# First products of a decoder trunk: modulation and weight parts spread over the engines in another way, and a planner with other costs

## The chip, the cores and the metric

The kernel runs on 1 core of one Trainium2 chip. A time is the device time of one execution in microseconds (us). The median of three runs before the change is 1367.15 us. The engines are PE (matrix products), DVE and POOL (elementwise vector work), ACT (activation functions, also copies with scale and bias) and SP, which issues the transfers (DMA).

## The reference

Two layers of a decoder over x (512 tokens by 1024 features, float32), then a last norm:

```python
mod = (c @ w_ada + b_ada)[:, None, :]
sh_m, sc_m, g_m, sh_f, sc_f, g_f = jnp.split(mod, 6, axis=-1)
h = rms_norm(x) * (1 + sc_m) + sh_m
proj = h @ w_in
x_lru, q_down, kv_down, k_rope, gate_a, gate_b = jnp.split(proj, IN_SPLIT_POINTS, axis=-1)
y_a = rg_lru(causal_depthwise_conv(x_lru, conv_w, conv_b), positions, ...)
y_b = mla(q_down, kv_down, k_rope, cos, sin, q_norm_g, kv_norm_g, w_uq, w_ukv)
y = jax.nn.sigmoid(gate_a) * y_a + jax.nn.sigmoid(gate_b) * y_b
x = x + g_m * (y @ w_out)
h = rms_norm(x) * (1 + sc_f) + sh_f
gate, up = jnp.split(h @ w_ffn_in, 2, axis=-1)
x = x + g_f * ((jax.nn.silu(gate) * up) @ w_ffn_out)
```

`rg_lru` is a gated recurrence over the tokens, `mla` a causal attention with 8 heads whose queries and keys come from narrow projections (`q_down` 256 columns, `kv_down` 128, `k_rope` 64). c is one vector of 1024, so `mod` is one vector of 6144 per layer: scale, shift and gate for both halves of a layer.

## The kernel before, in words

All activations lie feature-major: tile j holds 128 features by 512 tokens. Every product is done with operands split in two: a value is hi + lo, both in the engine's fast 32-bit type (`fp32r`), and `mm3` (line 567) issues three products of 128x512 per 128 rows of weights: hi by hi, hi by lo, lo by hi. `split` (line 558) makes the parts: ACT copies to hi, and a subtraction on DVE gives lo.

**Who sets the order.** The program doesn't issue its engine calls at once. A `Recorder` notes them, `order()` (line 302) plays them through on a model of the engines and lists for each engine, among the calls that are ready and have buffers, the one with the longest remaining path, and `issue()` issues them in that order (so every instruction carries line 503 before and 513 after). `cost()` (line 267) holds the durations of the model: a product of 512 columns, an elementwise step by its width, a transfer, an ACT table load. While the model's PE is idle before the first products are through, `fill()` puts in a product on zeros of 128x256 in bf16, the `fill` rows, whose results nobody reads. In the issued order each engine takes its instructions strictly in turn.

**The first products** (`first_products`, line 990). For the first layer the eight feature tiles of x are taken in order. Tile j needs `xn` (x times `rst`, the reciprocal root mean square of each token), its scale and shift, and the rows of `w_in` for x_lru tiles 0 and 1 and all narrow projections (704 columns). These are 17 products per tile into six accumulators, which stay open over all eight tiles. The scale and shift are made just before, for one or two tiles at a time, from the columns of `w_ada` that the tiles take (`first_mods`, line 948; 32 transfers of 256 KB into `wa`). The table `FIRST` has one entry per step: first tile, number of tiles, and two letters for scale and shift. Letter P: PE multiplies eight blocks of 128x128 of `wa` with c (`pt<-cols1,wa`, 128x64, in float32; each appears as two records). Letter V: DVE adds up the rows weighted by c (`wacc`: one `tensor_scalar` and seven `scalar_tensor_tensor` of 128x128 for one tile, 128x256 for two), and PE only sums over the partitions with one product per tile (`pt<-ones,wacc`). A small DVE step then adds the bias (`mod0_1` is the scale, `mod0_0` the shift).

`full_h` (line 998) turns `xn` into h: ACT writes the scaled and shifted tile once rounded (`hh`) and once in full (`xn`), and DVE subtracts (`hl`). `w_first` (line 618) loads and splits the weights: ACT writes `whi`, and the two subtractions (128x640 into `wlo`, 128x64 into a side column of `whi`) run on DVE for tile 0 and on POOL for tiles 1 to 7 (`WLO_G`). There are three raw weight buffers and three pairs of hi and lo.

**Beside and behind them.** `tables` (line 1058), placed after the third step, loads small parameters, makes the rotary tables (three steps of 128x512 on POOL) and `scol`, a chain of 22 steps of 128x16 on POOL with a reciprocal and one `scalar_tensor_tensor` (`w16_0`, in the trace `w`) on DVE. Then follow the statistics of the narrow projections (`sacc`, `rs2`), more columns of `w_in`, the convolution `xc`, the recurrence's gates and scans (`ri`), and the attention, interleaved by a script of steps (`SCRIPT`, line 75). In the background DVE adds up further modulation columns (`macc`, from `graw` transfers).

Of the kernel before, what the change touches and what calls it, by code (L numbers as in the profile page):

```python
# [78 lines left out]
FIRST = ((0, 1, "PP"), (1, 1, "VP"), (2, 2, "PV"), (4, 2, "VV"), (6, 2, "VV"))  # L79
A2_G = True  # L80
HI_G = ()
WLO_G = (1, 2, 3, 4, 5, 6, 7)
# [10 lines left out]

# [1 line left out]
# The body below records its engine calls in program order. order() then lists them by a  # L95
# simulated greedy schedule: each engine takes, of the calls whose operands are ready and whose
# tiles have a free buffer, the one with the longest remaining path. The calls are issued in
# that order, and Tile puts in the waits that the data needs.
# [17 lines left out]
class Op:  # L116
    __slots__ = ("eng", "call", "a", "k", "dur", "preds", "succs", "allocs", "tiles", "tail", "table", "idx",
                 "npred", "ready", "bytes", "live")


class Ref:
    """A view of a tile that is made when the first call on it is issued."""

    def __init__(self, root, steps, dtype, part, free, off):
        self.root, self.steps, self.dtype = root, steps, dtype
        self.part, self.free, self.off = part, free, off  # (start, count), [(stride, count)], column
# [67 lines left out]
class Recorder:  # L194
# [25 lines left out]
    def add(self, eng, real, method, a, k):  # L220
# [43 lines left out]
        op.dur = self.cost(op, eng, method, a, k, outs, ins)  # L264
        self.ops.append(op)

    def cost(self, op, eng, method, a, k, outs, ins):
# [8 lines left out]
        if eng == "PE":  # L276
            if method == "transpose":
                return 107.0
            lhs, rhs = a[1], a[2]
            n = free(rhs)  # L280
            op.live = n > 32
            return max(207.0, n * 1.667) if lhs.dtype == F32 else max(53.0, n * 0.417)
# [19 lines left out]
    def order(self):  # L302
# [8 lines left out]
        # longest remaining path, with the products chained in program order  # L311
# [14 lines left out]
        # users of each tile  # L326
# [12 lines left out]
        def fits(o):  # L339
            """a free buffer for each new tile, and one more for each tile that the program makes before it"""  # L340
# [17 lines left out]
        # the clock of the tensor engine: full speed after a window full of work, half after an idle one  # L358
# [21 lines left out]
        dma_free = 0.0  # L380
        res = []
# [8 lines left out]
        def fill():  # L390
            """keeps the clock of the idle tensor engine up until the first products are through"""
# [8 lines left out]
        while count < n:  # L400
            for e in ENGINES:
# [49 lines left out]
                if e == "PE":  # L451
                    d = clock(now, d, o.live)
                if e == "ACT" and o.table and table not in o.table:
                    d += TABLE_LOAD
                    table = o.table[0]
# [62 lines left out]
def trunk(  # L518
# [36 lines left out]
    def f(ap):  # L555
        return ap.bitcast(F32)
# [5 lines left out]
    def mm2(ps, wboth, xh, xl, start, stop):  # L562
        """high and low parts of 64 columns at once: their products lie in the two halves of the partitions"""
# [26 lines left out]
    def w_cols(src, nk=KD, on_g=False, raws=None):  # L590
        """src: rows (k p), 128 columns; gives [(hi, lo)] over k, and adds the blocks as loaded to raws"""
# [12 lines left out]
    def w_krope(l):  # L604
        """rotary key columns: high and low parts side by side"""
# [12 lines left out]
    def w_first(l, j, keep):  # L618
        """rows of feature tile j: columns of x_lru tiles 0 and 1 and of all the down projections; gives the
        five (hi, lo), the rotary key columns' high and low parts side by side, and the columns as loaded"""  # L620
# [23 lines left out]
    def w_lru(l, n0):  # L644
        """input and recurrence gate weights of blocks n0..n0+3"""
# [8 lines left out]
    def w_rope(l, g):  # L654
        """rotary query weights of heads 4g..4g+3, as [k][half][head, 32]"""
# [16 lines left out]
    def w_pair(l, p2):  # L672
        """query (no rotary) and key/value weights of heads 2*p2, 2*p2+1"""
# [49 lines left out]
    mods = {}  # L723

    def mod_steps(l, s):
        """generator: one segment (1024 columns) of c @ w_ada[l] + b_ada[l], as columns [128, 8]"""
# [25 lines left out]
    def mod_products(l, s):  # L752
        """the same segment on the tensor engine: w_ada stationary, c moving"""
# [21 lines left out]
    # ---- work for the tensor engine while it waits at the start, so that its clock stays up  # L775
# [32 lines left out]
    def rsqrt(r, ssum, n, w, eps):  # L808
        """r = (ssum / n + EPS) ** -0.5: the reciprocal of what the Sqrt table gives, and one Newton step"""
# [11 lines left out]
    def sqrt_eps():  # L821
        """EPS as a column by the Sqrt table, not before the last call so far: the table is there
        when the statistics are"""
# [6 lines left out]
    class Stat:  # L830
# [13 lines left out]
        def finish(self, cs, n, sbuf=False):  # L844
            """rstd broadcast over partitions, in columns cs of PSUM or of a tile in SBUF"""
# [26 lines left out]
    # Across a norm the products go on before its statistics are there: the first units take x times  # L872
    # the scale, and their results are multiplied by rstd and get the shift's share as a column.
    class Ahead:
# [12 lines left out]
        def units(self, srcs):  # L887
            """products with the column blocks srcs: PSUM tiles, and the shift's columns"""
# [21 lines left out]
    def gemm_units(units, xh, xl, get_w, done):  # L910
        """units: (m, column slice); weights of m by get_w(m): list over k of (hi, lo) APs"""
# [637 lines left out]
```

## Time and profile before

| | |
|---|---|
| runs | 1367.56, 1367.15, 1366.49 us; median 1367.15 us |
| profiled execution, span from first to last instruction | 1361.9 us |
| its own device time | not given beside the span; the median of the runs lies 5.25 us above it |
| mean granted PE clock | 0.995 of full speed |
| busy: PE, DVE, ACT, POOL | 98%, 64%, 46%, 16% of the span |
| instructions | 17108 |
| PE filler products | 57 |

PE is busy nearly all the time, so its rows show the run of the program from start to end: transposes of x to 16 us, the first products to 67 us, the first layer to about 680 us, the second to the end. A busy PE isn't at its peak everywhere: products overlap, and the distance from one start to the next says more than the duration of one. Idle time on another engine matters only where PE waits for what that engine makes. In timelines a row stands for one instruction or several of a kind in a row (x2, x3); the square brackets give the idle time just before it and what ended it.

### The profile page before, as it was taken

What the parts mean: (1) busy time and instruction counts of PE and PEld (TensorE: products, weight loads), DVE (VectorE), ACT (ScalarE), POOL (GpSimd) and SP (SyncE); (2) the same over time, 40 slices, a digit from 0 to 9 for tenths busy, and PEclk for the clock granted to TensorE, in tenths of its full rate; (3) what the DMA queues carried; (4) which work ended last, traced back from release to release, by engine and by line L of the source; (5) the groups of instructions that cost most, each with busy time, mean ns of one, the idle gap of its engine ahead of it and who ended that gap; (6) DMA issues with size and microseconds to landing.
All of it is one profiled execution on the core that took longest, in us unless ns stands there. A gap on an engine that the chain in (4) does not pass through costs nothing.

```text
span 1361.9 us, 17108 instructions
## 1 busy us (share of the span) xinstructions
PE 1339.6 (98%) x6330; PEld 1117.8 (82%) x6330; DVE 872.4 (64%) x1478; ACT 623.5 (46%) x963; POOL 213.2 (16%) x238
## 2 busy tenths in 40 slices
PE   8999989999999999999999999999999999999997
PEld 7788878887888888888888888888888888888887
DVE  5898799788856455556869887667673333333344
ACT  5585856644432222322356767855452322232223
POOL 1613334413000000000040243413400000000000
PEclk9999989999999999999999999999999999999999
DMA  9636344334655556555635333311433323433232
GB/s 300 200 96 168 103 124 140 124 117 137 194 182 164 163 159 206 178 170 184 203 86 141 92 86 100 94 47 47 124 89 98 89 75 104 120 93 95 77 88 81
DMA packets 251297, 174.92 MB, mean 128 GB/s; under 512 B 12767, under 2 KB 235341, under 8 KB 251213
## 3 DMA queue, kind: packets, MB, share of 16 engines
q1 hardware_dynamic: 251212, 173.82, 42.3%
q8 instruction: 50, 0.82, 0.2%
q14 instruction: 35, 0.28, 0.1%
HBM read 167.50 MB, written 2.10 MB: 125 GB/s over the span
## 4 chain that ended last, share of the span: by engine, by line
PE 84%; DVE 6%; DMA 5%; issue 2%; POOL 1%; ACT 1%; SPq 1%; ACTq 0%; DVEq 0%; POOLq 0%
PE mm L503 75%; PE s L503 4%; PE o L503 3%; DMA graw<-in_w_ada_dram 2%; PE pt L503 2%; DMA wa<-in_w_ada_dram 2%; DMA raw<-in_w_in_dram 1%; DVE macc L503 1%; DVE ri L503 1%; DVE wlo L503 1%; DVE xc L503 1%; POOL w L503 1%; DVE wacc L503 1%; SPq L503 1%; DVE sc L503 0%
## 5 line engine op out<-in xcount | busy, mean ns | idle before, releaser
L503 ACT ACTIVATE whi<-raw 128x1024 fp32r<-128x1024 f32 (+2 forms) x226 | 219.7, 973 | 581.3 <-PE mm L503 371.1
L503 DVE TENSOR_TENSOR wlo<-raw,whi 128x1024 fp32r<-128x1024 f32 (+2 forms) x218 | 249.3, 1145 | 205.5 <-ACT whi L503 201.2
L503 PE MATMUL mm<-fh,wlo 128*128 128x512 f32 x672 | 261.9, 390 | 0.0
L503 PE MATMUL mm<-fh,whi 128*128 128x512 f32 x672 | 261.7, 389 | 0.0
L503 PE MATMUL mm<-fl,whi 128*128 128x512 f32 x672 | 261.6, 389 | 0.0
L503 PE MATMUL mm<-hh,whi 128*128 128x512 f32 x408 | 161.3, 396 | 0.0
L503 PE MATMUL mm<-hl,whi 128*128 128x512 f32 x408 | 160.2, 393 | 0.0
L503 PE MATMUL mm<-hh,wlo 128*128 128x512 f32 x400 | 156.3, 391 | 0.0
L503 PEld LDWEIGHTS mm<-fl,whi 128*128 128x128 f32 x672 | 126.1, 188 | 26.4 <-DVE fl L503 0.2
L503 PEld LDWEIGHTS mm<-fh,wlo 128*128 128x128 f32 x672 | 126.1, 188 | 26.4 <-DVE wlo L503 0.3
L503 PEld LDWEIGHTS mm<-fh,whi 128*128 128x128 f32 x672 | 126.2, 188 | 26.0
L503 PE MATMUL mm<-ah,whi 128*128 128x512 f32 (+1 forms) x363 | 139.7, 385 | 0.0
L503 PE MATMUL mm<-ah,wlo 128*128 128x512 f32 (+1 forms) x363 | 139.3, 384 | 0.0
L503 PE MATMUL mm<-al,whi 128*128 128x512 f32 (+1 forms) x363 | 139.0, 383 | 0.0
L503 DVE SCALAR_TENSOR_TENSOR macc<-graw,cols,macc 128x512 f32<-128x512 f32 x140 | 103.8, 777 | 24.1 <-DMA graw<-in_w_ada_dram 23.7
L503 DVE TENSOR_TENSOR sg<-sg,mm 128x512 f32<-128x512 f32 x42 | 28.9, 688 | 111.1 <-PE mm L503 111.1
L503 PEld LDWEIGHTS mm<-hl,whi 128*128 128x128 f32 x408 | 77.0, 189 | 15.5 <-DVE hl L503 0.5
L503 PEld LDWEIGHTS mm<-hh,whi 128*128 128x128 f32 x408 | 77.0, 189 | 15.1 <-DVE whi L503 0.2
L503 PEld LDWEIGHTS mm<-hh,wlo 128*128 128x128 f32 x400 | 75.4, 189 | 15.8 <-POOL wlo L503 0.3
L503 PEld LDWEIGHTS mm<-ah,wlo 128*128 128x128 f32 x363 | 68.2, 188 | 13.3
L503 PEld LDWEIGHTS mm<-al,whi 128*128 128x128 f32 x363 | 68.2, 188 | 13.1
L503 PEld LDWEIGHTS mm<-ah,whi 128*128 128x128 f32 x363 | 68.2, 188 | 13.1
(266 smaller groups left out, 2173.9 us busy)
## 6 DMA issues: line engine op xcount, KB each, us to landing
raw<-in_w_ffn_in_dram SPq DMA_DIRECT2D x88, 512.0 KB, 3.9
graw<-in_w_ada_dram SPq DMA_DIRECT2D x80, 512.0 KB, 4.8
raw<-in_w_in_dram SPq DMA_DIRECT2D x49, 512.0 KB, 4.0
raw<-in_w_ffn_out_dram SPq DMA_DIRECT2D x32, 384.0 KB, 3.5
raw<-in_w_ffn_out_dram SPq DMA_DIRECT2D x32, 320.0 KB, 3.2
wa<-in_w_ada_dram SPq DMA_DIRECT2D x32, 256.0 KB, 5.6
raw<-in_w_out_dram SPq DMA_DIRECT2D x16, 512.0 KB, 3.9
raw<-in_w_uq_dram SPq DMA_DIRECT2D x24, 128.0 KB, 3.5
```

Of the source, the lines that this page charges most:

```text
L503: o.call(*(real(v) for v in o.a), **{k: real(v) for k, v in o.k.items()})
```

## The change

In `FIRST` the scale of step (1,1) and the shift of step (4,2) go from V to P, and in step (2,2) the two letters change places. `WLO_G` is empty, so all lo parts of the first weights are made on DVE. `full_h` makes the modulated tile in one DVE step with two column operands, then splits it as weights are split. The planner's costs of products are others, and a DVE or POOL step with two tensor inputs from SBUF now waits, in the model, for such a step on the other of the two. Comments and docstrings go, which moves line numbers only.

```diff
-FIRST = ((0, 1, "PP"), (1, 1, "VP"), (2, 2, "PV"), (4, 2, "VV"), (6, 2, "VV"))
+FIRST = ((0, 1, 'PP'), (1, 1, 'PP'), (2, 2, 'VP'), (4, 2, 'VP'), (6, 2, 'VV'))
...
-WLO_G = (1, 2, 3, 4, 5, 6, 7)
+WLO_G = ()
...
+        op.shared = eng in ("DVE", "POOL") and method in ("tensor_tensor", "scalar_tensor_tensor") and 2 == sum(
+            isinstance(x, Ref) and x.root.tag not in BANKS and x.shape[-1] > 1 for x in ins
+        )
...
-            return max(207.0, n * 1.667) if lhs.dtype == F32 else max(53.0, n * 0.417)
+            if lhs.dtype == F32:
+                return max(107.0, n * 1.667)
+            return n * 0.417 if lhs.dtype == BF16 else max(106.0, n * 0.417 + 10.3)
...
+        shared = {"DVE": 0.0, "POOL": 0.0}
...
+                if o.shared:
+                    other = "POOL" if e == "DVE" else "DVE"
+                    d += max(0.0, shared[other] - now)
+                    shared[e] = now + d
...
-            A.activation(hh[j], xn[j], AF.Identity, bias=sh, scale=sc)
-            A.activation(xn[j], xn[j], AF.Identity, bias=sh, scale=sc)
-            V.tensor_tensor(hl[j], xn[j], f(hh[j]), ALU.subtract)
+            V.tensor_scalar(xn[j], xn[j], sc, sh, ALU.mult, ALU.add)
+            split(hh[j], hl[j], xn[j])
```

By the tables PE has 64 modulation products of 128x64 instead of 40 and 8 of `ones` with `wacc` instead of 11; DVE has 32 `wacc` steps, all of 128x256, instead of 8 of 128x128 and 40 of 128x256. The planner makes the whole order anew. The filler products become 84 instead of 57, and ACT's table loads 56 instead of 51. Three places show what moves.

PE at the start of tile 1 (tile names: `hh_38`, `hl_46` are the parts of h, `mm_53` to `s_56` accumulators, `pt` the modulation's). Before:

```order
L503 MATMUL pt_81_371<-cols1_150,wa_85_265 128x64 x2
L503 MATMUL pt_81_371<-cols1_150,wa_82_234 128x64 x2
L503 MATMUL pt_81_371<-cols1_150,wa_83_240 128x64 x2
L503 MATMUL pt_81_371<-cols1_150,wa_84_252 128x64 x2
L503 MATMUL pt_81_371<-cols1_150,wa_85_265 128x64 x2
L503 MATMUL mm_53_345<-hh_38_363,whi_92_412 128x512
L503 MATMUL mm_53_345<-hl_46_390,whi_92_412 128x512
L503 MATMUL mm_53_345<-hh_38_363,wlo_93_425 128x512
L503 MATMUL mm_54_350<-hh_38_363,whi_92_412 128x512
L503 MATMUL mm_54_350<-hl_46_390,whi_92_412 128x512
L503 MATMUL pt_81_371<-ones_83,wacc_90_352 128x64 x2
L503 MATMUL mm_54_350<-hh_38_363,wlo_93_425 128x512
```

Now, where the first row shown is the last of 21 fillers that stand between the last products of tile 0 and tile 1:

```order
L513 MATMUL fill_4_87<-fill_x_75,fill_w_77 128x256
L513 MATMUL pt_80_458<-ones_83,wacc_85_360 128x64 x2
L513 MATMUL mm_53_365<-hh_38_400,whi_91_440 128x512
L513 MATMUL mm_53_365<-hl_46_418,whi_91_440 128x512
L513 MATMUL mm_54_369<-hh_38_400,whi_91_440 128x512
L513 MATMUL mm_54_369<-hl_46_418,whi_91_440 128x512
L513 MATMUL s_55_373<-hh_38_400,whi_91_440 128x512
L513 MATMUL mm_53_365<-hh_38_400,wlo_92_466 128x512
L513 MATMUL pt_80_458<-cols1_150,wa_86_257 128x64 x2
L513 MATMUL pt_80_458<-cols1_150,wa_87_267 128x64 x2
L513 MATMUL pt_80_458<-cols1_150,wa_88_283 128x64 x2
L513 MATMUL pt_80_458<-cols1_150,wa_89_302 128x64 x2
```

Before, 14 modulation products stood together ahead of the tile (seven rows of two, the last five are shown). Now fillers stand there, the two `ones` products (one row) have moved ahead of the tile, and 16 modulation products for the shift of tiles 2 and 3 (eight rows, four of them shown) come after its sixth product. The lo parts that POOL's queue held before stand on DVE among its `wacc` steps, and POOL's queue begins with the rotary tables.

DVE behind the first products, before (`w16_0` is the step that needs the chain on POOL, `sacc` the statistics that PE waits for next):

```order
L503 SCALAR_TENSOR_TENSOR xc_172_784<-xl_171_769,cols2_638,xc_172_784 128x510
L503 SCALAR_TENSOR_TENSOR w16_0_643<-w16_4_71,w16_0_643 128x16
L503 SCALAR_TENSOR_TENSOR xc_172_784<-xl_171_769,cols2_638,xc_172_784 128x509
L503 TENSOR_TENSOR sacc_148_810<-sacc_148_810,sq_149_815 128x512
L503 TENSOR_TENSOR xcl_174_836<-xc_172_784,xch_173_829 128x512
L503 TENSOR_TENSOR wlo_204_851<-raw_202_747,whi_203_840 128x1024
```

Now:

```order
L513 SCALAR_TENSOR_TENSOR xc_170_801<-xl_169_786,cols2_685,xc_170_801 128x509
L513 TENSOR_TENSOR sacc_146_825<-sacc_146_825,sq_147_831 128x512
L513 TENSOR_TENSOR wlo_202_855<-raw_200_767,whi_201_844 128x1024
L513 TENSOR_TENSOR xcl_172_875<-xc_170_801,xch_171_862 128x512
L513 RECIPROCAL rs2_149_897<-hs_150_870 128x4
L513 TENSOR_SCALAR ms_151_902<-o_148_859 128x4
L513 RECIPROCAL rs2_160_904<-hs_161_894 128x4
L513 SCALAR_TENSOR_TENSOR nt_152_907<-rs2_149_897 128x4
L513 TENSOR_SCALAR ms_162_909<-o_159_867 128x4
L513 SCALAR_TENSOR_TENSOR nt_163_911<-rs2_160_904 128x4
L513 TENSOR_TENSOR nt_152_907<-nt_152_907,ms_151_902 128x4
L513 SCALAR_TENSOR_TENSOR w16_0_692<-w16_4_71,w16_0_692 128x16
```

The step on `w16_0` stands no longer ahead of `sacc`, but ten rows behind it, among the statistics `rs2`.

DVE around 175 us of the trace before (`ri<-a2` are elementwise steps of the recurrence, `ri<-a` with `a` the scans, `xc<-mm` the convolution, which frees an accumulator of PE, `macc` the background modulation). Before:

```order
L503 SCALAR_TENSOR_TENSOR macc_169_1270<-graw_388_1825,cols1_150,macc_169_1270 128x512 x2
L503 SCALAR_TENSOR_TENSOR ri_258_1235<-a2_390_1850,ri_258_1235 128x512
L503 TENSOR_TENSOR xcl_382_1886<-xc_380_1828,xch_381_1878 128x512
L503 TENSOR_SCALAR sg_354_1847<-sg_354_1847 128x512
L503 SCALAR_TENSOR_TENSOR ri_212_1082<-a_383_1806,ri_212_1082 128x512
L503 SCALAR_TENSOR_TENSOR xc_395_1889<-mm_394_1823,cols2_638,xc_395_1889 128x511
L503 SCALAR_TENSOR_TENSOR ri_255_1228<-a_364_1656,ri_255_1228 128x512
L503 SCALAR_TENSOR_TENSOR xc_395_1889<-mm_394_1823,cols2_638,xc_395_1889 128x510
L503 TENSOR_TENSOR wlo_476_1917<-raw_474_1864,whi_475_1901 128x1024
L503 SCALAR_TENSOR_TENSOR xc_395_1889<-mm_394_1823,cols2_638,xc_395_1889 128x509
```

Now:

```order
L513 SCALAR_TENSOR_TENSOR xc_378_1868<-mm_377_1790,cols2_685,xc_378_1868 128x510
L513 SCALAR_TENSOR_TENSOR ri_256_1267<-a2_388_1873,ri_256_1267 128x512
L513 SCALAR_TENSOR_TENSOR xc_378_1868<-mm_377_1790,cols2_685,xc_378_1868 128x509
L513 SCALAR_TENSOR_TENSOR macc_167_1374<-graw_386_1862,cols1_150,macc_167_1374 128x512 x2
L513 TENSOR_TENSOR xcl_380_1934<-xc_378_1868,xch_379_1917 128x512
L513 SCALAR_TENSOR_TENSOR xc_393_1910<-mm_392_1860,cols2_685,xc_393_1910 128x511
L513 TENSOR_TENSOR wlo_474_1955<-raw_472_1883,whi_473_1922 128x1024
L513 SCALAR_TENSOR_TENSOR xc_393_1910<-mm_392_1860,cols2_685,xc_393_1910 128x510
L513 SCALAR_TENSOR_TENSOR ri_210_1110<-a_381_1803,ri_210_1110 128x512
L513 SCALAR_TENSOR_TENSOR xc_393_1910<-mm_392_1860,cols2_685,xc_393_1910 128x509
```

The two scans ahead of the last `xc` of tile `xc_395` have become one, of another tile, between its last two parts; the other has gone further back.

## Rows read from the trace of the kernel before

**Rows 1.** The page, part 1: busy time, share of the span, instructions of each engine.
```profile
PE 1339.6 (98%) x6330; PEld 1117.8 (82%) x6330; DVE 872.4 (64%) x1478; ACT 623.5 (46%) x963; POOL 213.2 (16%) x238
```

**Rows 2.** Three windows: busy us and instructions by engine, PE's granted clock, DMA share and rate.
```profile
core 0: us, PE busy (x) PEld busy (x) DVE busy (x) ACT busy (x) POOL busy (x), PEclk, DMA share, GB/s
28.50:46.50 18.00, 15.80 (x82) 11.85 (x81) 18.00 (x40) 8.42 (x13) 6.20 (x7) 1.00 0.92 287
184.00:191.00 7.00, 6.47 (x16) 4.34 (x15) 7.00 (x13) 5.21 (x7) 2.71 (x2) 0.52 0.86 284
1100.00:1150.00 50.00, 50.00 (x222) 41.39 (x221) 15.95 (x21) 10.64 (x14) 0.00 (x0) 1.00 0.31 89
```

**Rows 3.** PE's waits, 0 to 350 us: waited for, us in total, times, longest.
```profile
PE mm L503 <- DVE xc L503: 3.0, 1, 3.0
PE pt L503 <- DVE cols L503: 2.1, 1, 2.1
PE pt L503 <- DVE mod L503: 2.1, 2, 1.8
...
PE o L503 <- DVE sacc L503: 1.0, 1, 1.0
```

**Rows 4.** Groups on DVE, then POOL, 20 to 76 us: busy us, mean ns, idle before.
```profile
L503 DVE SCALAR_TENSOR_TENSOR wacc<-wa,cols,wacc 128x256 f32<-128x256 f32 x35 | 22.9, 700 | 0.1
...
L503 DVE TENSOR_TENSOR wlo<-raw,whi 128x640 fp32r<-128x640 f32 x1 | 0.8, 818 | 0.0
...
L503 DVE TENSOR_SCALAR ang<-ang 128x512 f32<-128x512 f32 x1 | 0.4, 446 | 0.0
...
L503 POOL TENSOR_SCALAR kk<-kk 128x512 f32<-128x512 f32 x1 | 0.9, 941 | 0.1
```

**Rows 5.** Timeline of DVE, then POOL, around 27 us: start, duration.
```profile
26.55 0.48 DVE L503 SCALAR_TENSOR_TENSOR wacc<-wa,cols,wacc 128x256 f32<-128x256 f32 x1
...
27.54 1.77 DVE L503 SCALAR_TENSOR_TENSOR wacc<-wa,cols,wacc 128x256 f32<-128x256 f32 x1
...
27.34 1.70 POOL L503 TENSOR_TENSOR wlo<-raw,whi 128x640 fp32r<-128x640 f32 x1 [26.51 <-ACT whi L503]
```

**Rows 6.** PE's timeline at places in the first products and behind them.
```profile
20.98 0.71 PE L503 MATMUL mm<-hh,whi 128*128 128x512 f32 x2
...
25.43 3.23 PE L503 MATMUL pt<-cols,wa 128*128 128x64 f32 x28
28.47 0.48 PE L503 MATMUL mm<-hh,whi 128*128 128x512 f32 x1
...
45.01 1.70 PE L503 MATMUL fill<-fill_x,fill_w 128*128 128x256 bf16 x14
...
52.88 0.66 PE L503 MATMUL pt<-ones,wacc 128*128 128x64 f32 x4 [2.15 <-DVE cols L503]
...
67.15 0.48 PE L503 MATMUL mm<-hh,whi 128*128 128x512 f32 x1
...
75.99 1.03 PE L503 MATMUL s<-ident,rs 128*128 128x128 f32 x8
```

**Rows 7.** Timeline of POOL, then DVE: scol's chain and the step that waits for it.
```profile
58.00 0.54 POOL L503 TENSOR_TENSOR w<-w,w 128x16 f32<-128x16 f32 x1
...
69.63 0.18 DVE L503 SCALAR_TENSOR_TENSOR w<-w,w 128x16 f32<-128x16 f32 x1 [1.41 <-POOL w L503]
```

**Rows 8.** DVE's timeline, 163 to 184 us.
```profile
164.69 1.75 DVE L503 SCALAR_TENSOR_TENSOR macc<-graw,cols,macc 128x512 f32<-128x512 f32 x2 [2.03 <-DMA graw<-in_w_ada_dram]
...
175.61 2.30 DVE L503 TENSOR_TENSOR_SCAN ri<-a,ri 128x512 f32<-128x512 f32 x1
...
182.16 0.73 DVE L503 SCALAR_TENSOR_TENSOR xc<-mm,cols,xc 128x509 f32<-128x509 f32 x1
```

**Rows 9.** ACT, 740 to 960 us: its table loads (groups), then its longest wait.
```profile
L503 ACT ACT_TABLE_LOAD x24 | 30.8, 1283 | 0.7 <-DVE mx L503 0.3
...
ACT whi L503 <- PE mm L503: 23.7, 18, 2.5
```

More of the change, by code (lines that the diff above doesn't have):

```diff
@@ L117 @@
     __slots__ = ("eng", "call", "a", "k", "dur", "preds", "succs", "allocs", "tiles", "tail", "table", "idx",
-                 "npred", "ready", "bytes", "live")
+                 "npred", "ready", "bytes", "live", "shared")
 class Ref:
```

## The prediction

> **What bounds the kernel now.** I read the page's busy times first, then PE's waits, then windows, then the timelines of PE, DVE and POOL. PE is busy for 98% of the span [rows 1], so time can come only from PE's own work, its few waits, its filler products and the stretches in which it runs at a lower clock. In an undisturbed window of the feed-forward part PE starts 222 products in 50 us, 0.225 us each [rows 2]; that is the unit below (the 0.39 us that a timeline prints for one is its latency). The waits [rows 3] are few: 2.1 us for `cols`, 2.1 for `mod` and 1.0 for `sacc` in the first 76 us, and one of 3.0 us for `xc` at 180 us. After this last one the window from 184 to 191 us shows a granted clock of 0.52, that is 1.2 instead of 2.4 GHz, and 16 products in 7.00 us [rows 2]: 16 x 0.225 = 3.6 us of work and 0.5 us of idle time, so 2.9 us lost to the clock. Everything after 350 us is PE without a wait worth naming; the change can gain only at the start and around 180 us.
>
> In the first products DVE is what holds PE. It is busy all of the 18.0 us from 28.5 to 46.5 us [rows 2]. One wacc step of 128x256 takes 0.48 us, but 1.77 us when POOL's lo part of 1.70 us stands beside it [rows 5], and the mean of 35 is 700 ns [rows 4]: 35 x (700 - 480) = 7.7 us too much, six such collisions of 1.3 us. PE's wait of 2.15 us ends at 52.88 us with a DVE copy [rows 6] that stood behind such a row of slow steps.
>
> **The sum** is made on the profiled execution (span 1361.9 us); the median of the runs, 1367.15 us, lies 5.25 us above it, and I take that as the part around the span, which the change leaves alone. About 0.2% (2.7 us) is what a measurement of this kernel can tell from no change.
>
> *Work on PE.* The table gives 64 modulation products instead of 40, and 8 products of `ones` with `wacc` instead of 11. Fourteen modulation products stand between 25.43 and 28.47 us, 3.04 us, so one costs 0.217 us [rows 6]; 24 more cost 5.2 us, three `ones` products fewer give 0.65 back. On the path: +4.6 us, if PE is the bound.
>
> *Work on DVE.* Eight wacc steps of 128x128 and eight of 128x256 go. The latter are 0.48 us each (0.40 from start to start), the former have half the columns and I take 0.27: in all about 5.4 us. The collisions give their 7.7 us back. Added are seven lo parts of 128x640 (0.82 us each, 0.74 from start to start) and seven of 128x64 (a tenth of the columns, 0.14 as I take it), 6.1 us, and eight `tensor_scalar` of 128x512. None of these with two columns is in the trace; the nearest row is the clamp of `ang`, 0.446 us [rows 4]. Bounds: 0.38, that row's pitch, and 0.82, what the two-input lo part of 640 columns takes. I take 0.39, so 3.1 us. DVE's net is -5.4 - 7.7 + 6.1 + 3.1 = about -4 us: it stops being the bound, and PE becomes it.
>
> *First products, as a replay.* `rst`, `xn` and now one `tensor_scalar` stand before tile 0's first `hh`, which before could start with ACT; a lo part lies between too. I put tile 0 at 22.2 us instead of 20.98 [rows 6], so it ends at 26.1 with the 17 products as before, less the modulation products that stood among them. Then the new order has 21 fillers (14 took 1.70 us [rows 6], 0.115 each start to start, 2.4 us) and two `ones` products: tile 1 starts at 28.95 us against 28.47. From there PE has 7 x 17 = 119 products (26.8 us), 32 modulation products (6.9), 6 of `ones` (1.3), two transposes and four fillers (0.7): 35.7 us, and ends at 64.7; with small gaps 64.95. Before, the next stage starts at 67.15 us [rows 6]. Gain 2.2 us. Is the work there in time? My list of DVE's durations ends `hl` of tile 7 near 58 us, where PE needs it near 61; the w_ada blocks are loaded in the same order. Bounds of the term: 0, if half of the waits stay, and 4, if DVE lets the fillers be all the idle time.
>
> *The statistics after it.* DVE's step on `w` waited 1.41 us for the POOL chain of `scol`, which ran on it from 58.00 us until the step could start at 69.63 [rows 7], and `sacc` stood behind it: PE's wait of 1.0 us. In the new order the step stands behind `sacc`. Gain 1.0 us; what is late next is that chain: it starts after a reciprocal that comes about 7 us later, and if it again takes 11.6 us it holds the `rs` statistics, which PE used at 75.99 us [rows 6], for 1 to 2 us. Bounds of the term: a loss of 1.0 and a gain of 1.0. Fewer ACT steps (one of the two affine steps of each tile is now a plain copy, the other goes) cost and gain nothing: ACT's idle time there covers them.
>
> *At 180 us.* PE waits for the last `xc` of a tile, which frees an accumulator. DVE had waited 2.03 us for a weight transfer at 164.69 us, then did two scans, the first of 2.30 us, ahead of the last `xc` at 182.16 us [rows 8]. In the new order only one scan stands there, and one `ri` step goes ahead of the wait for the transfer, so that it falls into it. The scan of 2.30 us alone is 2.2 us from start to start. The wait shrinks from 3.0 to at most 0.8 us: -2.2. A wait of 1.8 us at the start and the one of 1.0 are followed by full clock, those of 2.15 and 3.0 us by half clock; so I expect no fall: -2.9. Together -5.1, bounds 0 and -5.9.
>
> Sum: -2.2 - 1.0 - 2.2 - 2.9 = -8.3, **1358.9 us**.
>
> A rule weighed. In the rows a two-input step beside a two-input POOL operation waits it out, 1.77 instead of 0.48 us. The Trainium skill, "SBUF — State Buffer", section "Who interferes with whom", says so too (the loser of the shared port pair fully blocks), but says it also of a VectorE `tensor_scalar` in a 2-port mode against any GpSimd operation. No row here shows that. By that rule the new `tensor_scalar` of tiles 6 and 7 could each wait for a POOL table step such as `kk`, up to 0.94 us [rows 4], and the sum would be up to 1.9 us less good, 1360.8; the new scheduler counts only the two-input kind.
>
> **Rivals.**
> 1. *The start gains, the middle does not.* The wait for `xc` moves to another place: for it speaks that the whole order is made anew, with POOL's steps beside the scans, against it the shorter list ahead of `xc`. -3.2: **1364.0 us**.
> 2. *The start gives nothing.* PE pays the +4.6 us and DVE is late all the same, as modulation now waits for PE and PE for DVE; the two waits of 1.8 and 2.15 us stay. That is -2.2 + 1.8 + 2.15 = +1.7, less 1.0 for `sacc`: **1367.9 us**. For it: DVE is full until 46.5 us. Against: DVE's work falls by 4 us.
> 3. *Slower: table loads.* The new order has 56 activation table loads instead of 51, two more in the first layer's heads and three in the second's. In the stretch 740 to 960 us 24 of them take 1283 ns each [rows 9]. If each delays a step that PE waits for, 5 x 1.28 = 6.4 us, less 3.2 of the start: **1370.4 us**. It decides from the point where ACT's lag is more than PE's buffers hold; three paid and one fall of the clock (3.8 + 2.9 - 3.2 = +3.5) give the same. Against it: ACT waited 23.7 us for PE in that stretch to write weights [rows 9], so it is ahead mostly. A queue that is late at another place, with a clock fall behind it, ends at about the same time.
>
> **How the numbers follow.** Forecast 0.42, rival 1 0.27, rival 2 0.14, rival 3 0.17. The forecast and two thirds of rival 1 are faster by over 0.2%: 0.60; the rest of rival 1 and rival 2 are within it: 0.23; slower 0.17. The range goes from 1356.5 (the start term at its better bound) to 1370.5, which takes in all rivals; the likeliest case alone has 1356.5 to 1361.5.
>
> **What would show it.** Right: no wacc step over 0.6 us between 27 and 50 us; the next stage's first product at 65 us; no PE wait over 1 us from 28 to 76 us; the wait at 180 us under 1 us and a clock of 1.00 from 180 to 192. Wrong: a wait of PE for `mod` or `hl` of 2 us or more in the first products; a new window at about half clock; PE waits in 740 to 960 us that end with ACT.

## The result and the profile after

| | before | changed |
|---|---|---|
| median of the runs | 1367.36 us (4 runs, 1366.49 to 1367.81) | 1374.78 us (4 runs, 1373.74 to 1375.65) |
| ratio of the runs | | 1.006, 95% interval 1.0045 to 1.0074 |
| span of the profiled execution | 1361.9 us | 1372.0 us |
| PE filler products, ACT table loads | 57, 51 | 84, 56 |

The changed kernel is slower by 7.4 us between the medians; the ratio of the runs is 1.006. The forecast was 1358.9 us in a range up to 1370.5. The changed kernel's profiled execution took 1373.74 us for a span of 1372.0 us, so 1.7 us lie around the span, not 5.25; in all other runs on record it is 1.7 to 2.1 us. The execution profiled of the kernel before must then have lain about 3.5 us below the median of its runs, and of the 10.1 us between the two spans only some 7.4 are to be counted.

The page of the changed kernel, part 1 (busy time, share, instructions):

```profile
PE 1345.9 (98%) x6399; PEld 1124.9 (82%) x6399; DVE 874.3 (64%) x1484; ACT 623.3 (45%) x960; POOL 188.6 (14%) x224
```

PE has 6.3 us more busy time than before [rows 1] and is at 98% again: such a share shows neither kernel's loss. Where it arises shows when the same product is taken from PE's timeline of both kernels:

| product on PE | before, us | changed, us | difference |
|---|---|---|---|
| first one behind the first products | 67.15 | 67.06 | -0.1 |
| first one of the recurrence's gates | 75.76 | 74.44 | -1.3 |
| transposes (`pt<-ident,sc`) ahead of the wait for `xc` | 176.01 | 176.11 | +0.1 |
| first `s<-xch,lwh` behind that wait | 197.83 | 196.85 | -1.0 |
| first of the output projection, layer 1 | 286.48 | 287.95 | +1.5 |
| last `mm<-yh,whi` of the output projection, layer 1 | 331.94 | 335.32 | +3.4 |
| `rs` of the next norm | 340.02 | 348.12 | +8.1 |
| first product on the normed tile (`mm<-fh,whi`) | 347.03 | 353.48 | +6.4 |
| last `mm<-fh,whi`, in the middle of the feed-forward part | 636.40 | 642.56 | +6.2 |
| `rs` of the second layer's first norm | 703.41 | 711.44 | +8.0 |
| first of the output projection, layer 2 | 943.49 | 953.36 | +9.9 |
| end of the span | 1361.9 | 1372.0 | +10.1 |

The start is a little faster, and the loss comes behind it: 2.8 us up to the output projection of layer 1, 1.9 us in that projection, 3.0 us around the second norm up to the first `fh` product, and two smaller steps of about 1.8 us, one at the end of the first layer and one in the second. PE's longest waits, first from 0 to 360 us, then from 360 us to the end (in total, times, longest):

```profile
PE o L513 <- DVE sacc L513: 3.0, 1, 3.0
PE pt L513 <- DVE rwl L513: 2.0, 1, 2.0
PE o L513 <- DVE mred L513: 2.0, 1, 2.0
PE mm L513 <- DVE xc L513: 1.4, 1, 1.4
PE o L513 <- DVE pl L513: 1.3, 1, 1.3
```

```profile
PE o L513 <- DVE mred L513: 1.4, 1, 1.4
```

Before, the longest waits in this stretch were those of 3.0 us for `xc` and 2.1 us for `cols` and `mod` [rows 3]. The waits for `cols` and `mod` are gone and the one for `xc` has shrunk; others of 1.3 to 3.0 us stand farther on. `rwl` is the lo part of rotary query weights. `mred` is DVE's last step on a segment of the background modulation: PE waits for it at 320.93 us and once more, 1.43 us, at 680.22 us. Three windows tell of the clock (busy us and instructions of PE, PEld, DVE, ACT, POOL; granted clock; DMA):

```profile
184.00:191.00 7.00, 4.96 (x22) 3.72 (x21) 7.00 (x7) 3.73 (x7) 3.38 (x2) 0.99 0.01 4
190.50:194.00 3.50, 3.46 (x10) 2.85 (x11) 3.18 (x4) 0.00 (x0) 0.00 (x0) 0.55 0.21 42
344.00:348.40 4.40, 4.40 (x17) 3.54 (x17) 1.25 (x7) 1.32 (x2) 0.00 (x0) 0.61 0.43 120
```

From 184 to 191 us, where the kernel before had a clock of 0.52 [rows 2], it is 0.99 now. The fall isn't gone, it has moved: from 190.5 to 194 us, right behind the wait for `rwl`, the clock is 0.55. A second one is new: from 344 to 348.4 us, right behind the wait for `sacc`, it is 0.61, part of the time at 1.2 GHz. Not every wait of this length has one behind it: after the 2.0 us for `mred` the clock is 1.00 from 320 to 330 us.

The start in detail, PE's timeline (start, duration, product):

```profile
20.10 1.04 PE L513 MATMUL fill<-fill_x,fill_w 128*128 128x256 bf16 x8
...
21.81 0.38 PE L513 MATMUL fill<-fill_x,fill_w 128*128 128x256 bf16 x2
...
22.87 1.36 PE L513 MATMUL fill<-fill_x,fill_w 128*128 128x256 bf16 x11
23.99 0.70 PE L513 MATMUL mm<-hh,whi 128*128 128x512 f32 x2
...
27.97 2.47 PE L513 MATMUL fill<-fill_x,fill_w 128*128 128x256 bf16 x21
...
30.64 0.48 PE L513 MATMUL mm<-hh,whi 128*128 128x512 f32 x1
...
67.06 0.48 PE L513 MATMUL mm<-hh,whi 128*128 128x512 f32 x1
```

Between 18 and 24 us stand 16 modulation products and 21 fillers (8, 2 and 11) ahead of tile 0, which begins at 23.99 us instead of 20.98 [rows 6]. Another 21 fillers stand behind it, and tile 1 begins at 30.64 instead of 28.47. DVE's groups from 18 to 76 us:

```profile
L513 DVE SCALAR_TENSOR_TENSOR wacc<-wa,cols,wacc 128x256 f32<-128x256 f32 x28 | 12.8, 481 | 0.0
...
L513 DVE TENSOR_SCALAR xn<-xn,mod,mod 128x512 f32<-128x512 f32 x8 | 4.6, 589 | 0.0
```

A wacc step takes 481 ns on the mean instead of 700 [rows 4]: the collisions with POOL are gone. The new step with two columns takes 589 ns on the mean.

How much the start gains hangs on which execution of the kernel before is taken. The kernel before_sums below has the instruction order of the kernel before up to 300 us. In its trace PE waits longer for `sacc`, the clock falls behind the wait, and the first product of the gates stands at 79.52 us:

```profile
73.28 1.96 PE L502 MATMUL o<-ones,sacc 128*128 128x1 f32 x16 [2.29 <-DVE sacc L502]
...
79.52 0.40 PE L502 MATMUL s<-xch,lwh 128*128 128x512 f32 x1
```

The window from 72 to 80 us, first of the kernel before, then of before_sums:

```profile
72.00:80.00 8.00, 8.00 (x45) 6.85 (x45) 6.76 (x17) 7.27 (x13) 0.00 (x0) 1.00 0.52 143
```

```profile
72.00:80.00 8.00, 6.72 (x32) 5.73 (x33) 5.50 (x16) 5.01 (x8) 0.69 (x1) 0.79 0.36 83
```

So one order has this product at 75.76 us in one execution and at 79.52 in another. The changed order has it at 74.44, 74.23 and 74.20 us in three traces (its own, sums_late, sums_mid), with no wait for `sacc`. By these traces the start gains from 1.3 to 5.3 us, and the profiled pair shows the low end.

The largest loss stands at 337 us. DVE, then POOL, then PE:

```profile
337.12 5.70 DVE L513 TENSOR_TENSOR wlo<-raw,whi 128x1024 fp32r<-128x1024 f32 x1 [0.16 <-ACT whi L513]
342.74 0.68 DVE L513 TENSOR_TENSOR sacc<-sacc,sq 128x512 f32<-128x512 f32 x1
```

```profile
337.01 2.53 POOL L513 TENSOR_TENSOR wsa<-wsa,wsb 128x512 f32<-128x512 f32 x2
339.50 2.23 POOL L513 TENSOR_TENSOR wsa<-wsa 128x256 f32<-128x256 f32 x4
```

```profile
343.48 1.05 PE L513 MATMUL o<-ones,sacc 128*128 128x1 f32 x8 [3.00 <-DVE sacc L513]
344.39 0.71 PE L513 MATMUL mm<-xw,whi 128*128 128x512 f32 x1
```

A lo part of 128x1024 takes 5.70 us on DVE; one at 331.68 us took 1.40. While it runs, POOL does six two-input sums back to back (`wsa`, shift columns for the next norm), from 337.01 to 341.73 us, and the lo part ends 1.09 us after the last of them, about what it takes when alone. `sacc` stands behind it on DVE, PE waits 3.0 us for `sacc`, and its next products run at the lower clock.

### The profile page after: what moved, and what is told of

It is laid out like the page before. It is cut to its first block, busy times and chain, and to the rows that moved or that the text cites. A ratio compares the mean times of both kernels' runs of the same rounds, so it can differ in the third digit from the quotient of the medians.

```text
span 1372.0 us, 17233 instructions
## 1 busy us (share of the span) xinstructions
PE 1345.9 (98%) x6399; PEld 1124.9 (82%) x6399; DVE 874.3 (64%) x1484; ACT 623.3 (45%) x960; POOL 188.6 (14%) x224
## 4 chain that ended last, share of the span: by engine, by line
PE 71%; DVE 4%; DMA 2%; ACT 2%; issue 1%; POOL 0%; ACTq 0%; DVEq 0%
PE mm L513 66%; PE s L513 2%; DMA graw<-in_w_ada_dram 2%; PE o L513 2%; PE pt L513 1%; DVE macc L513 1%; ACT whi L513 1%; DVE wlo L513 0%; ACT L513 0%; DVE ri L513 0%; DVE mred L513 0%; ACT ri L513 0%; DVE yt L513 0%; POOL sc L513 0%; DVE t L513 0%
## 5 line engine op out<-in xcount | busy, mean ns | idle before, releaser
L513 DVE TENSOR_TENSOR wlo<-raw,whi 128x1024 fp32r<-128x1024 f32 (+2 forms) x225 | 259.0, 1152 | 213.6 <-ACT whi L513 212.4
```

What stands on the lines that cost most here:

```text
L513: o.call(*(real(v) for v in o.a), **{k: real(v) for k, v in o.k.items()})
```

## The experiments

The experiments stand in four groups, each with the kernel before on the same chip; its medians there were 1366.5, 1365.9, 1366.8 and 1366.3 us, with single executions from 1362.2 to 1372.2 us, so a time is compared with that of the kernel before in its own group. The changed kernel was timed apart from the four groups, at a ratio of 1.0060 (1.0045 to 1.0074); where another kernel is set against it, the ratios count, and a difference in us between them is rough.

**Which half of the change loses: the program or the planner?** The first kernel keeps the three edits of the program and gives the planner its old numbers; the second does the opposite; the third and fourth take the changed kernel and undo one part of the planner's change. The lines show what becomes of the changed kernel.

```diff
  old_planner: the program of the change, and
-                return max(107.0, n * 1.667)
-            return n * 0.417 if lhs.dtype == BF16 else max(106.0, n * 0.417 + 10.3)
+            return max(207.0, n * 1.667) if lhs.dtype == F32 else max(53.0, n * 0.417)
-                if o.shared:
+                if False:
  new_planner_only: FIRST, WLO_G and full_h as before, the planner of the change
  no_shared: the change with the last pair alone
  old_cost: the change with the pair of costs alone
```

> The three edits of the program (FIRST, WLO_G, full_h) with the planner of before (old costs, no shared rule). If the loss is made by the order that the planner's new numbers give behind the first products, this is below the kernel before, 1363 to 1366 us, with the start as in the changed kernel (sacc product near 70 us) and no wait over 2 us at 300 to 350 us. If the edits of the program make the loss, it stays at 1373 to 1376. If any new order is a draw, it lies between or outside, with waits at places that neither kernel has.

> The program of before with the new planner (new costs, shared rule). If the planner's numbers make the loss: 1373 to 1377 us with waits in the middle of the first layer. If the edits of the program make it: 1366 to 1368. If any new order is a draw: neither.

> The changed kernel without the planner's rule that a two-input step of DVE or POOL waits for the other. If this rule moves steps so that the long wait of DVE behind POOL near 337 us (one lo part of 5.70 instead of 1.22 us) comes about: 1367 to 1370 us. If the rule is not what counts: 1373 to 1376, with a DVE lo part or sum over 4 us there again.

> The changed kernel with the old costs of products (the shared rule stays). If the costs of products make the loss (a model in which a float32 product of 64 columns costs half of the 0.217 us that it takes): 1367 to 1370 us. If not: 1373 to 1376.

| | time, us | ratio to before, 95% interval |
|---|---|---|
| old_planner | 1364.88 | 0.9986 (0.9968 to 1.0005) |
| new_planner_only | 1384.40 | 1.0110 (1.0077 to 1.0143) |
| no_shared | 1384.52 | 1.0118 (1.0088 to 1.0147) |
| old_cost | 1372.19 | 1.0039 (1.0024 to 1.0055) |

The planner's numbers make the loss: with the old ones the edits of the program are no slower than before, and with the new ones the program of before loses 15 to 18 us (by the ratio and by the medians). My guesses on the two parts of the planner's change both fell. Without the shared rule the changed kernel is not better but some 8 to 10 us worse; with the rule and the old costs it is slower than with neither, and not told from the changed kernel (1.0024 to 1.0055 against 1.0045 to 1.0074). The parts don't add, and the waits are at other places in each. Two of these kernels have their longest wait where the changed kernel has none, at the first attention scores, for a key or query that ACT writes (no_shared, then new_planner_only):

```profile
116.93 1.43 PE L513 MATMUL s<-kh,qh 128*128 128x512 f32 x4 [4.79 <-ACT kh L513]
```

```profile
122.78 1.44 PE L513 MATMUL s<-kh,qh 128*128 128x512 f32 x4 [4.07 <-ACT qh L513]
```

**Is it what the numbers say, or that there is another order at all?** Two kernels take the costs apart, without the shared rule; three others nudge a number of the kernel before, the cost of a product by 0.7% up or down or that of a DVE step by 2 ns, which means nothing in itself.

```diff
  f32_half: the program of the change, no shared rule, and only
+                return max(107.0, n * 1.667)
+            return max(53.0, n * 0.417)
  f32r_long: the same, and only
+                return max(207.0, n * 1.667)
+            return n * 0.417 if lhs.dtype == BF16 else max(106.0, n * 0.417 + 10.3)
  nudge_pe: the kernel before, and
-            return max(207.0, n * 1.667) if lhs.dtype == F32 else max(53.0, n * 0.417)
+            return max(207.0, n * 1.667) if lhs.dtype == F32 else max(53.0, n * 0.420)
  nudge_dve: the kernel before, and
-            return 68.0 + n * 1.042 + 62.0 * min(cols, 1)
+            return 70.0 + n * 1.042 + 62.0 * min(cols, 1)
  pe_down (in the next group): the kernel before with 0.414 for 0.417
```

> The changed program, no shared rule, and of the costs only the float32 one changed (a small float32 product 107 instead of 207; the 128x512 products stay at 213.5). If this number, half of the 0.217 us that such a product takes, makes the loss: 1375 to 1386 us. If it is harmless: 1363 to 1367, as with the old planner. If any new order is a draw: anywhere from 1363 to 1386, and not to be told from the number changed.

> The changed program, no shared rule, and only the cost of the 128x512 products changed (223.8 instead of 213.5, nearer to the 225 ns that they take). If a cost of PE below the true one served the old order as a margin, so that the feeding engines were planned early: 1375 to 1386 us. If the exact number is harmless: 1363 to 1367. If any new order is a draw: anywhere from 1363 to 1386.

> The kernel before with one planner number nudged by 0.7% (0.417 to 0.420 ns a column of a product), which has no meaning of its own. If any new order is a draw around a tuned one: 2 to 15 us slower than before, 1369 to 1382. If the new numbers as such do the harm: within 2 us of before, 1364.5 to 1368.5.

> The kernel before with another planner number nudged (2 ns on a DVE step, under 1% of most). The same expectations: 1369 to 1382 us if any new order is a draw around a tuned one, 1364.5 to 1368.5 if the new numbers as such do the harm.

> The kernel before with the planner's product cost nudged down by 0.7% (0.417 to 0.414 ns a column). If any new order is a draw around a tuned one: 2 to 15 us slower, 1368 to 1381. If a cost of PE below the true one is a margin that helps: 1362 to 1367.

| | time, us | ratio to before, 95% interval |
|---|---|---|
| f32_half | 1366.70 | 1.0005 (0.9994 to 1.0015) |
| f32r_long | 1381.05 | 1.0110 (1.0095 to 1.0125) |
| nudge_pe | 1373.42 | 1.0055 (1.0040 to 1.0070) |
| nudge_dve | 1369.20 | 1.0023 (1.0011 to 1.0035) |
| pe_down | 1369.53 | 1.0016 (1.0002 to 1.0030) |

The float32 cost, half the time of the product it stands for, leaves the program no slower than the kernel before. Against old_planner, from which f32_half differs by this number alone, it loses about 0.2% (0.9994 to 1.0015 against 0.9967 to 0.9993 in the longer row of old_planner below), at the edge of what the runs can tell. The cost of the 128x512 products, which is nearer to the 0.225 us that they take [rows 2], loses 1.1% alone, nearly all that both costs lose together (no_shared). But a nudge of 0.7% of that same number already costs 0.55%, as much as the whole change, a nudge down costs 0.16%, and a nudge of 2 ns on DVE steps 0.23%. So the sign of an edit to the planner isn't read from whether the number becomes truer: the nine orders that other planner numbers gave lose something between nothing and 18 us, and the old numbers' orders are among the best of those tried. In nudge_pe's trace, for one, the clock is 0.61 from 72 to 80 us and 0.64 from 116 to 124 us, where it is 1.00 in that of the kernel before. That the old order was chosen among many would explain why it is good; no run shows it. Whether a short PE cost is also a margin that helps stays open: down and up by 0.7% both lose, up loses more.

**The fillers, and POOL's sums.** The next two keep the changed order and take out one thing.

```diff
  few_fill, in issue():
+                n += o.idx == self.fill
+                if o.idx == self.fill and n > 37:
+                    continue
  sums_late, in Ahead.units and issue(); GV has POOL's place in the plan and DVE's engine:
+                E = GV if (self.l, self.ssh) == (0, SH_F) else G
-                G.tensor_tensor(a, a, b, ALU.add)
+                E.tensor_tensor(a, a, b, ALU.add)
  and so for the two sums that follow; issue() holds these back until the next `ht` step on DVE or a call that needs them
```

> The changed kernel in the changed order, but the last 47 of its 84 filler products (those from 20 us on, 5 us of PE's queue ahead of and behind tile 0) are not issued. If the fillers stand in the way of products whose operands are ready: the next stage's first product at 63.5 to 65.5 us instead of 67.06, and 1371 to 1373 us. If they only fill time in which the operands are late: 66.5 to 67.5 us there, waits of PE for mod, hh or hl in their place, and 1374 to 1376.

> The changed kernel in the changed order, but six sums of shift columns ahead of the first layer's second norm run on DVE behind that norm's statistics, not on POOL beside DVE's lo part at 337 us. If POOL's back-to-back two-input steps hold DVE there: the lo part takes 1.2 us instead of 5.70, PE's wait for sacc of 3.0 us goes, so does the half clock from 344 to 348 us, and it is 1370 to 1373 us. If something else stretches the lo part: over 4 us again and 1374 to 1376.

few_fill: 1372.87 us, ratio 1.0037 (1.0021 to 1.0054); the interval overlaps that of the changed kernel, so a gain in the whole isn't shown. PE's timeline of it:

```profile
23.05 0.74 PE L517 MATMUL mm<-hh,whi 128*128 128x512 f32 x2 [0.32 <-ACT hh L517]
...
29.37 0.63 PE L517 MATMUL pt<-ones,wacc 128*128 128x64 f32 x4 [2.11 <-DVE wacc L517]
```

```profile
66.07 0.48 PE L517 MATMUL mm<-hh,whi 128*128 128x512 f32 x1
```

Tile 0 starts at 23.05 us instead of 23.99, and before tile 1 PE waits 2.11 us for `wacc` where 21 fillers stood; the next stage starts at 66.07 us instead of 67.06. So neither expectation fits: of some 5 us of fillers 1 us stood in the way, and the rest filled time in which DVE was late.

sums_late: 1371.89 us, ratio 1.0031 (1.0017 to 1.0045). DVE's timeline, and PE's waits from 325 to 360 us:

```profile
336.42 1.23 DVE L521 TENSOR_TENSOR wlo<-raw,whi 128x1024 fp32r<-128x1024 f32 x1 [0.16 <-ACT whi L521]
...
348.08 1.29 DVE L519 TENSOR_TENSOR wsa<-wsa,wsb 128x512 f32<-128x512 f32 x2
```

```profile
PE o L521 <- DVE wsa L519: 2.5, 1, 2.5
```

The lo part takes 1.23 us, so POOL's sums were what held it. PE's wait for `sacc` and the lower clock from 344 to 348.4 us are gone, but the sums come at 348 us, too late: PE waits 2.5 us for them, and the clock falls behind this wait instead:

```profile
350.00:354.00 4.00, 3.70 (x11) 3.12 (x12) 4.00 (x9) 1.65 (x3) 0.00 (x0) 0.52 0.02 6
```

In this profiled execution the gain is given back at the next place; over the runs the ratio is 1.0031, its interval just meeting that of the changed kernel. The following three put the sums right behind the last step of the norm's statistics, in the changed kernel, in the kernel before and in old_planner; the edit is that of sums_late, with `rs2` as the place.

> The changed kernel with the six sums of shift columns on DVE right behind the last step of the norm's statistics (in the last trial they came too late, and PE waited 2.5 us for them). If POOL's hold on DVE was worth what the trace shows (3.0 us of wait and about 1.7 us of half clock): 1369.5 to 1371.5 us, no PE wait over 1 us from 330 to 355 us. If the gain is given back at the next norm or in the feed-forward part again: 1371.5 to 1373.

> The same move in the kernel before, where POOL's sums stretch three small steps of the statistics (0.58, 1.20 and 0.65 us for 128x4) and PE waits 1.46 us for rs. If POOL holds DVE there too: that wait is gone and it is 1364.5 to 1366 us. If not: within 0.5 us of before, with the wait.

> The three edits of the program with the old planner, and the same move of the sums. If the two gains add: 1362.5 to 1364 us, 0.2 to 0.35% below the kernel before. If they don't: 1364 to 1366.

| | time, us | ratio to before, 95% interval |
|---|---|---|
| old_planner once more | 1364.68 | 0.9980 (0.9967 to 0.9993) |
| sums_mid | 1370.53 | 1.0023 (1.0011 to 1.0036) |
| before_sums | 1365.05 | 0.9985 (0.9972 to 0.9999) |
| old_planner_sums | 1362.99 | 0.9974 (0.9960 to 0.9989) |

The first of these belongs to the group before:

> The three edits of the program with the old planner once more, for a narrower interval. If the edits are worth their predicted start gain of 3.2 us in a body like the old one: 0.3 to 0.4% below the kernel before, clear of it. If the gain is given back by fillers and other waits: within 0.2%.

It is 2.1 us below its kernel before, 0.07 to 0.33%: clear of it, and short of the 0.3% named. sums_mid has a ratio of 1.0023 where the changed kernel has 1.0060, and the intervals don't meet: the move takes some 4 us off. From 325 to 360 us, the window of the changed kernel and that of sums_mid:

```profile
325.00:360.00 35.00, 32.00 (x143) 26.18 (x142) 28.05 (x41) 16.72 (x23) 12.19 (x22) 0.95 0.29 91
```

```profile
325.00:360.00 35.00, 34.87 (x160) 28.10 (x159) 29.37 (x51) 19.31 (x26) 7.51 (x16) 1.00 0.33 103
```

The clock goes from 0.95 to 1.00 and PE starts 160 products instead of 143. In the kernel before the same sums stretched three steps of 128x4, whose last held `rs` and PE; first as it was, with PE's product, then in before_sums:

```profile
337.47 0.58 DVE L503 SCALAR_TENSOR_TENSOR nt<-rs 128x4 f32<-128x4 f32 x1
338.09 1.20 DVE L503 TENSOR_TENSOR nt<-nt,ms 128x4 f32<-128x4 f32 x1
339.32 0.65 DVE L503 SCALAR_TENSOR_TENSOR rs<-nt,rs 128x4 f32<-128x4 f32 x1
```

```profile
340.02 0.65 PE L503 MATMUL s<-ident,rs 128*128 128x128 f32 x4 [1.46 <-DVE rs L503]
```

```profile
339.64 0.16 DVE L502 SCALAR_TENSOR_TENSOR nt<-rs 128x4 f32<-128x4 f32 x1
339.83 0.16 DVE L502 TENSOR_TENSOR nt<-nt,ms 128x4 f32<-128x4 f32 x1
340.03 0.16 DVE L502 SCALAR_TENSOR_TENSOR rs<-nt,rs 128x4 f32<-128x4 f32 x1
340.11 1.28 DVE L502 TENSOR_TENSOR wsa<-wsa,wsb 128x512 f32<-128x512 f32 x2
```

Each of the three steps takes 0.16 us when POOL is quiet, and the wait of 1.46 us is gone. old_planner_sums is 0.26% below the kernel before (0.11 to 0.40%) and beats both kernels. That is in line with the gains of the edits (0.20%) and of the sums (0.15%) adding, but it isn't told from the edits' gain alone, so that they add isn't shown. Its two longest waits that are left, from 76 to 1000 us:

```profile
PE mm L510 <- DVE xc L510: 3.7, 1, 3.7
PE s L510 <- ACT kh L510: 2.7, 1, 2.7
```

## Why the prediction was wrong, point by point

- *DVE is relieved.* Right: wacc steps of 481 instead of 700 ns, and no wait of PE for `mod` or `cols`. The step with two columns, taken as 0.39 us from start to start, was mis-sized but inside its bounds of 0.38 to 0.82: 0.46 us from start to start for six of the eight, which print 0.54.
- *The rule weighed.* The other two, for tiles 6 and 7, took 0.63 and 0.83 us. They ran beside `tensor_scalar` steps of POOL; DVE's rows, then POOL's:

```profile
57.77 0.63 DVE L513 TENSOR_SCALAR xn<-xn,mod,mod 128x512 f32<-128x512 f32 x1
...
58.32 0.83 DVE L513 TENSOR_SCALAR xn<-xn,mod,mod 128x512 f32<-128x512 f32 x1
```

```profile
57.37 0.75 POOL L513 TENSOR_SCALAR ang<-pos,ct 128x512 f32<-128x512 f32 x1 [56.54 <-ACT w L513]
58.21 0.66 POOL L513 TENSOR_SCALAR kk<-ang 128x512 f32<-128x512 f32 x1
```

  Each of the two ends 0.28 us behind the end of a POOL step (58.12 and 58.87 us). That agrees with the Trainium skill, "SBUF — State Buffer", section "Who interferes with whom", which has a VectorE step in a 2-port mode wait for the whole of a GpSimd instruction that started first. Whether the step ran in such a mode no row shows. It cost 0.4 us on DVE, where up to 1.9 was named, and PE didn't wait for it.
- *First products, -2.2 us.* Failed at one step: "I put tile 0 at 22.2 us instead of 20.98". It began at 23.99 us, since 16 modulation products and 21 fillers stand ahead of it in PE's order; I had counted the fillers behind tile 0 only. few_fill shows that about 1 us of the miss was fillers and the rest late operands. The replay from tile 1 on was good: 36.0 us named, 36.4 measured. The gain of the stage was 0.1 us instead of 2.2 in the profiled pair, and up to 1.2 us against before_sums, which ends the stage at 68.02 us, with 66.81 in sums_mid.
- *The statistics, -1.0 us.* Right in kind: the wait for `sacc` there is gone, and at 75 us the kernel is 1.3 us ahead in the pair. Against before_sums, where this wait is 2.29 us with a lower clock behind it, it would be over 5. The step on `w` waited 1.31 us for POOL's chain, as feared, but PE had other work:

```profile
74.59 0.18 DVE L513 SCALAR_TENSOR_TENSOR w<-w,w 128x16 f32<-128x16 f32 x1 [1.31 <-POOL w L513]
```

- *At 180 us, -5.1 us.* Half of the mechanism was right. Only one scan, of 1.2 us, stands ahead of the last `xc`, as foreseen, and the wait is 1.4 us instead of 3.0 ("at most 0.8" was named). But "I expect no fall" failed: one scan and the background modulation went behind `xc`, PE waits 2.0 us for `rwl` at 190.5 us, and the clock is 0.55 right behind it. The table's two rows at 176 and 197 us show 1.1 us gained over this stretch in all.
- *The step that decided* was the sum's silence on the rest: "Everything after 350 us is PE without a wait worth naming; the change can gain only at the start and around 180 us." It can lose anywhere, since the planner makes the whole order anew. I compared the orders at places of a wait that was there and none at places where a wait could come. There the runs show new waits: 2.0 us for `rwl`, 2.0 and 1.4 us for `mred`, 3.0 us for `sacc`, two of them with a fall of the clock. From 1.3 us ahead at 75 us the changed kernel falls to 10.1 behind, 11.4 us in the profiled pair. The rival that foresaw a moved wait ("The start gains, the middle does not") gave it the size of the old one. The nearest was the last sentence under rival 3, "A queue that is late at another place, with a clock fall behind it": this is what came, at more than one place; the time, 1374.78 us, lies above the 1370.4 given there.
- *Rival 3, table loads.* Right in sign, wrong in cause. There are 27 loads instead of 24 in the stretch of the second layer, but PE's waits there are at most 0.6 us, and those that ACT ends are 0.7 us together:

```profile
PE mm L513 <- ACT ri L513: 0.4, 1, 0.4
...
PE o L513 <- ACT ph L513: 0.3, 1, 0.3
```

- *The size around the span*, 5.25 us: wrong, it is 1.7 to 2.1 us for each run; the profiled execution before lay about 3.5 us below the median. A slip in the range: the start term at its better bound of 4 gives 1357.1 us, not 1356.5.
- The gain at the start, forecast as 3.2 us in rival 1: with the old planner the program's edits gain 1.6 and 2.1 us over the whole run. The first of the two isn't clear of zero, the second lies between 0.07 and 0.33%, 1 to 4.5 us, which takes in 3.2. The planner's new numbers lose more than that behind the start.

What stays open: the steps at 252 us (`kl`, `kh`), at 321 and 680 us (`mred`, 2.0 and 1.4 us) and in the second layer were not taken apart one by one; they are told from waits alone. Only the one at 337 us was removed by an experiment.

## What to carry to other kernels

A change to a planner's costs is a change to every place of the program, also where the profile shows no wait now: price it as a new draw of the order, with the spread of a few meaningless nudges of the same numbers, before the truth of a number is taken as a gain. Compare a new order with the old at the narrow places (norm statistics, first users of a late tile), not only where there is a wait to lose. And where a two-input POOL step can run beside DVE, look at the train that it stands in: six short ones in a row cost a DVE step beside them 4.5 us here, and moving them to DVE gained in the changed kernel and in the kernel before; in old_planner the difference is within the noise.

## What was not expected of the hardware

- A DVE step of 128x1024 was held through six POOL steps in a row (5.70 us, and 5.70 and 5.72 us in few_fill and no_shared), although POOL's steps are separate instructions. In the kernel before, steps of 128x4 ended after one POOL step each (0.58, 1.20, 0.65 us). Why the small ones came through between and the wide one didn't is open. The planner's shared rule counts only the rest of the one step that runs.
- POOL's `tensor_scalar` with one tensor input, just ahead of these sums, cost a two-input DVE step little: a lo part took 1.40 instead of 1.23 us, and the `hl` step at 59.9 us 0.96 instead of 0.69.
- Executions of one unchanged kernel differ by up to 10 us on one chip (1362.2 to 1372.2 us for the kernel before in the first group), more than the whole effect of this change; a single profile stands for one of them. The spread goes with the granted clock: in the third group the executions of the kernel before at 0.994 or more took 1362.2 to 1366.8 us, those at 0.991 or less 1369.3 to 1371.0 (in the first group the two go together less closely). The two traces of one order at 72 to 80 us, above, show a place where it arises.
